# Warming TensorE on three float32 products and two gate products, with other cuts of the first two chunks

## The chip, the cores and the metric

The kernel runs on one core of one Trainium2 chip. The metric is the device time of one execution in microseconds. A product here is one matrix instruction of TensorE; the profile calls TensorE PE, VectorE DVE, ScalarE ACT, GpSimd POOL and SyncE SP.

## The reference

`x` has the shape (16, 2048, 1024), `w` (1024, 1024) and `decay` (1024), all float32. The kernel computes a matrix product and then a decaying running sum along the second axis:

```python
xw = x @ w
out[:, 0, :] = xw[:, 0, :]
for t in range(1, S):
    out[:, t, :] = decay[None, :] * out[:, t - 1, :] + xw[:, t, :]
```

## The kernel before

The 16 x 2048 rows of `x` are cut into 64 chunks of 512 rows (`TL`), and a chunk into 16 blocks of 32 rows (`NJ`). GpSimd's queue loads `x` in bfloat16 into tiles `xb`, one DMA for each of the four quadrants of 32 partitions (a quarter of the 1024 columns each). VectorE turns blocks of 32 x 32 pairs into `xw` (`turn`, L115), ScalarE or VectorE sorts them into `xt` (`part`, L123), and TensorE multiplies `xt`, or `xw` directly, with the weights `wsb` (`matmul`, L131). The products go to PSUM tiles `ps` and `spare`; the scan, the decays and the transposition back to the output follow on VectorE, ScalarE and GpSimd.

The work is a list of 264 steps, each of them one output tile: up to two chunks by 128 of the 1024 output columns. A table called `agenda` says which small pieces of work are issued in which step. Everything is pinned, so each engine runs its instructions in the order of the program. The entry -99 of the agenda is the beginning, before step 0. Its letters that matter here are `M` (load part of a chunk of `x`, `load_half`), `U` (load a part of `w`), `K` (`spin_on`), `E` (turn one part of a chunk), `F` and `G` (sort it), `w` and `W` (convert a piece of the weights into `wsb`, L326).

Chunks 0 and 1 are loaded, turned and multiplied in two parts each, so that TensorE can begin before a whole chunk has landed. `cuts` holds the borders: nine and seven blocks for chunk 0, eight and eight for chunk 1. For chunk 0, 32 products of 288 columns are followed by 32 of 224. The order on GpSimd's queue is: first part of chunk 0 (four DMAs), a quarter of `w`, the second part of chunk 0, chunk 1's two parts, the rest of `w`.

Before the first data are there, TensorE multiplies a cleared tile `idle` with itself, into the PSUM tile `spare`, whose content is overwritten later: 22 products at L344. After these come the gates: for each quadrant, ScalarE copies one landed column of `xb` into a cleared tile `gate` (L360), and TensorE multiplies with that gate three times (once for the last quadrant). Because of the copy, these products can't run before the quadrant's load has landed. The real products are queued behind them.

From step 40 to step 139 a no-op stands on TensorE's queue ahead of the products of each step.

Of the kernel before, what the change touches and what calls it, by code (L numbers as in the profile page):

```python
# [9 lines left out]
FP32 = mybir.dt.float32  # L10
BF16 = mybir.dt.bfloat16
# [14 lines left out]
def kernel(  # L26
# [26 lines left out]
    nc = tc.nc  # L53
    pin = tc.keep_in_program_order
    B, S, D = x.shape
    assert w.shape == (D, D)

    NQ = 4
    P = 32
# [3 lines left out]
    TL = 512  # L63
    NJ = TL // P
# [5 lines left out]
    const = ctx.enter_context(tc.tile_pool(name="const", bufs=1))  # L70
# [5 lines left out]
    def ring(pool, name, count, shape, dtype=FP32):  # L76
        i = turns[name] = turns.get(name, -1) + 1
        return pool.tile(shape, dtype, name=f"{name}{i % count}")

    def quad(q):  # L80
        return slice(q * P, (q + 1) * P)
# [17 lines left out]
    xt_of = {}  # L99
# [25 lines left out]
    def matmul(ps, n, k, xt, t0=0, t1=TL, start=0, pairs=None):  # L125
        if pairs is None:
            rhs = xt[:, k // 2, k % 2, t0:t1]
        else:
            rhs = pairs[:, k // 2, t0 // P:t1 // P, :, k % 2].rearrange("p j i -> p (j i)")
        lhs = wsb[:, k, n].rearrange("p q i -> p (q i)")  # L130
        pin(nc.tensor.matmul(  # L131
            out=ps[:, t0:t1] if ps.shape[1] >= t1 else ps,
            lhsT=lhs,
            rhs=rhs,
            start=(k == 0 and t0 == start),
            stop=(k == K - 1),
        ))
# [179 lines left out]
    def load_w(queues, h, e):  # L317
        for i, q in enumerate((0, 2, 1, 3)):
            pin(queues[i % len(queues)].dma_start(  # L319
                out=stage[h, e][quad(q)].rearrange("p (m d) -> p m d", m=M),  # L320
                in_=_ap(w, [[2 * D, P], [2 * P * D, M], [1, CH]],
                        (q * CQ + e) * D + h * CH)))
# [3 lines left out]
        pin(copy(out=wcols[:, 2 * m + e, h],  # L326
                 in_=src.rearrange("p (q r i) -> p q r i", q=NQ, r=R)))

    idle = const.tile([128, TL], BF16, name="idle")
    spare = ring(psp, "spare", 1, [128, TL])  # L330
    rows = const.tile([128, 2, P], FP32, name="rows")
    touch = const.tile([128, 1], BF16, name="touch")
    load_w((nc.sync, nc.scalar), 0, 0)
    pin(nc.vector.memset(idle, 0.0))  # L334
    pin(nc.vector.memset(rows, 0.0))
    pin(nc.scalar.copy(out=touch, in_=idle[:, 0:1]))

    gates = [const.tile([128, 128], BF16, name=f"gate{q}") for q in range(NQ)]
    for gate in gates:
        pin(nc.vector.memset(gate, 0.0))  # L340

    def spin(count, by):
        for _ in range(count):
            pin(nc.tensor.matmul(out=spare, lhsT=by, rhs=idle, start=True, stop=True))  # L344

    spin(22, idle[:, 0:128])
    H = NJ // 2
    cuts = (((0, H + 1), (H + 1, NJ)), ((0, H), (H, NJ)))
    for q in range(NQ):
        pin(nc.sync.dma_start(  # L350
            out=rows[q * P:q * P + R],
# [6 lines left out]

    def spin_on(q):
        pin(nc.scalar.copy(out=gates[q][quad(q), 0:1], in_=xb_of[0][quad(q), 0, 0:1]))  # L360
        spin(3 if q < NQ - 1 else 1, gates[q])

    def load_part(i):
        load_w((nc.gpsimd,), *((0, 1), (1, 0), (1, 1))[i])
# [42 lines left out]
    def finale():  # L407
        six, six_late = ring(psp, "ps", 3, [128, TL]), ring(psp, "ps", 3, [128, TL])
        seven, seven_late = ring(psp, "spare", 1, [128, TL]), ring(psp, "ps", 3, [128, TL])
        return tuple((early[:, 0:TL // 2], late[:, TL // 2:TL])  # L410
                     for early, late in ((six, six_late), (seven, seven_late)))

    def half_of(n, half, ks=range(K)):
        ps = finals[n % R - 2][half]
        t = half * (TL // 2)
        for k in ks:
            matmul(ps, n, k, xt_of[nch - 1], t, t + TL // 2, t)
# [49 lines left out]
    def turn_and_load(c):  # L467
# [40 lines left out]
        "L": lambda i: load(*loads.pop(0)) if loads else None,  # L508
    }
    agenda = {  # L510
        -99: "M0 U0 M1 M2 M3 U1 U2 w0 W1 w2 W3 K0 K1 K2 K3 E0 E1 G0 E2 G1 E3 F2 G3 W4 w5 W6 W7 D E4 E5 G4 E6 G5 E7 F6 G7 E8 E9 G8 E10 G9 E11 F10 G11 E12 L E13 G12 L E14 G13 E15 L F14 G15",
        0: "p0 z0 W8 W9 W10 W11",
        1: "g0",
        2: "L S1 L",
# [62 lines left out]
    def usual(s):  # L577
        paired = [t.paired for t in tiles]
        do = [f"P{s}"] if paired[s] else []
        if paired[s - 1]:  # L580
            do.append(f"S{s - 1}")
        if not paired[s]:
            do.append(f"S{s}")
        do.append(f"C{s - 1}")
        if paired[s - 2]:
            do.append(f"B{s - 2}")
        if not paired[s - 1]:
            do.append(f"B{s - 1}")
        return do + later.get(s, []) + ["L"] * (2 if len(loads) > NQ else 1)

    def rest(s):
        do = [f"S{s - 1}"] if tiles[s - 1].paired else []
        do.append(f"C{s - 1}")
        if tiles[s - 2].paired:
            do.append(f"B{s - 2}")
        return do + [f"B{s - 1}"] + later.get(s, []) + ["L"] * len(loads)

    def perform(do):
        for deed in do:
            deeds[deed[0]](int(deed[1:] or 0))  # L600
# [3 lines left out]
    for step, (g, n) in enumerate(slots):  # L604
        T = TL * len(g)
        left = step - len(slots)
        if n % R == 0:
            ns, nj = range(n, n + R), T // P
            if left == -2 * R:
                outlets = [Outlet(ns, H, half) for half in range(2)]  # L610
            else:
                pieces = 1 if left < -7 * R else 2 if left < -6 * R else nj // H
                outlets = [Outlet(ns, nj, pieces=pieces)]
        if left == -R:
            outlets = []
        if step == 0:
            heads = [ring(psp, "ps", 3, [128, T]) for _ in range(3)]
            firsts = [ps[:, 0:TL] for ps in heads] + [spares[0]]
            seconds = [ps[:, TL:T] for ps in heads] + [spares[1]]
            for j0, j1 in cuts[0]:  # L620
                for e in range(2):
                    for k in range(e, K, 2):
                        for i in range(R):
                            matmul(firsts[i], i, k, xt_of[0], j0 * P, j1 * P, j0 * P,
                                   pairs=None if e else xw_of[0])
            for k0 in range(0, K, 2):
                for i in range(R):
                    for k in (k0, k0 + 1):
                        matmul(seconds[i], i, k, xt_of[1], 0, H * P,
                               pairs=xw_of[1] if k0 < 4 else None)  # L630
            for i in range(R):
                for k in range(K):
                    matmul(seconds[i], i, k, xt_of[1], H * P, TL, H * P,
                           pairs=xw_of[1] if i < 2 else None)
        if step < R:
            ps = heads[n] if n < 3 else tuple(spares)
        else:
            if step == K + 1:
                ps = nexts
            elif left >= -2:  # L640
                finals = finals if left == -1 else finale()
                ps = finals[left + 2]
            elif len(g) == 2 or n % R < 3:
                ps = ring(psp, "ps", 3, [128, T])
            else:
                ps = ring(psp, "spare", 1, [128, TL])
            todo = [(k, l) for k in range(K) for l in range(len(g))]
            if step < K:
                todo.sort(key=lambda kl: kl[0] % 2)
            elif step == K:  # L650
                todo = []
                nexts = (ring(psp, "spare", 1, [128, TL]), ring(psp, "ps", 3, [128, T])[:, TL:T])
                for l in range(len(g)):
                    for i, one in enumerate((ps[:, l * TL:(l + 1) * TL], nexts[l])):
                        for k in range(K):
                            matmul(one, n + i, k, xt_of.get(g[l]),
                                   pairs=xw_of[g[l]] if l or not i and k >= M else None)
            elif step == K + 1:
                todo = []
            if left == -2:  # L660
                for m, half in ((n, 0), (n + 1, 0), (n, 1)):
                    half_of(m, half)
            if left >= -2:
                todo = []
            if 40 <= step < 140:
                pin(nc.tensor.nop(hint="room", nofuse=True))
            for k, l in todo:
                matmul(ps[:, l * TL:(l + 1) * TL], n, k, xt_of[g[l]])
        tiles.append(Tile(g, n, ps, outlets))
        do = agenda.get(step, agenda.get(left) if left >= -20 else None)  # L670
        if do is None:
            do = usual(step)
        else:
            do = do.split()
            if left == -20:
                do = rest(step) + do
        perform(do)
# [29 lines left out]
```

## Time and profile before

| | us |
|---|---|
| median of 3 runs | 904.14 |
| lowest and highest | 903.82, 904.59 |
| the profiled execution's own time | 903.76 |
| its span, from first to last instruction | 902.0 |
| first real product starts | 10.80 |
| last operation of TensorE ends | 897.94 |

| engine | busy us | share of the span |
|---|---|---|
| PE | 896.6 | 99% |
| DVE | 824.3 | 91% |
| ACT | 686.7 | 76% |
| POOL | 657.0 | 73% |

The span begins with the first instruction that the profile holds. Products overlap: one of 512 columns has a length of 0.379 us in the profile, but the next one starts 0.216 us after it. So the distance between starts is what says how fast TensorE works, and "busy" alone does not. A line of the timeline gives start, length, engine, line of the kernel, operation, what is written and read, the number of instructions merged, and in brackets the idle time of the engine ahead of it with what ended it. The granted clock is TensorE's, as a share of its full speed.

### The profile page before, as it was taken

The page shows a single profiled execution, that of the slowest core. Times are in us where ns is not written, and L with a number is a line of the kernel's source. Part 1 is how long each engine was busy: PE and PEld are TensorE (multiplying, and loading weights), DVE is VectorE, ACT ScalarE, POOL GpSimd, SP SyncE. Part 2 cuts the span into 40 slices and gives each one's busy share as a digit, 9 for nine tenths or more (in the row PEclk, how much of TensorE's full clock was granted, in tenths as well). Part 3 has the DMA queues.
Part 4 walks back from the last instruction along what each step waited for, and adds up shares of the span by engine and source line. Part 5 has one row for each costly group of instructions (what it writes and reads, how often), then busy time and mean ns, then how long its engine had stood idle before and what let it go on. Part 6 is the DMA issues. An engine that isn't in the chain of part 4 may idle for free.

```text
span 902.0 us, 12287 instructions
## 1 busy us (share of the span) xinstructions
PE 896.6 (99%) x4224; PEld 413.6 (46%) x4224; DVE 824.3 (91%) x633; ACT 686.7 (76%) x961; POOL 657.0 (73%) x756
## 2 busy tenths in 40 slices
PE   9999999999999999999999999999999999999998
PEld 6444444444444444444444444444444444444444
DVE  4999998998999999999998999999999999999998
ACT  4889867777877877878778778777787787787743
POOL 7988678777767768677677687777777776876532
PEclk9999999999999999999999999999999999999999
DMA  9999999999999999999999999999999999999858
GB/s 193 188 215 215 226 249 214 217 220 241 252 243 261 245 251 249 251 253 237 224 234 228 224 230 225 236 225 227 233 230 227 230 231 223 227 226 220 181 143 237
DMA packets 403182, 204.77 MB, mean 227 GB/s; under 512 B 9392, under 2 KB 402096, under 8 KB 403120
## 3 DMA queue, kind: packets, MB, share of 16 engines
q1 hardware_dynamic: 265808, 134.77, 60.7%
q0 software_dynamic: 137024, 68.70, 56.8%
q8 instruction: 33, 0.54, 0.2%
q10 hardware_dynamic: 288, 0.52, 0.2%
q14 instruction: 29, 0.24, 0.1%
HBM read 138.42 MB, written 134.22 MB: 302 GB/s over the span
## 4 chain that ended last, share of the span: by engine, by line
PE 98%; DMA 1%; POOL 0%; issue 0%; DVE 0%; DVEq 0%; POOLq 0%
PE ps L131 97%; DMA xb<-in_x_dram 1%; PE spare L131 1%; POOL xb L105 0%; PE spare L404 0%; PE ps L404 0%; DVE h L425 0%; DVE xw L115 0%; DVEq L702 0%; DVEq L115 0%; POOLq L691 0%
## 5 line engine op out<-in xcount | busy, mean ns | idle before, releaser
L131 PE MATMUL ps<-xt,wsb 128*128 128x512 bf16 (+1 forms) x4032 | 866.0, 377 | 0.0
L131 PEld LDWEIGHTS <-wsb 128*128 128x128 bf16 x4176 | 408.1, 98 | 477.3 <-ACT wsb L326 1.3
L205 POOL TENSOR_TENSOR xs<-h,xs 128x512 f32<-128x512 f32 (+1 forms) x190 | 242.7, 1278 | 185.5 <-ACT h L171 84.9
L278 DVE STREAM_TRANSPOSE ot<-so 128x1024 f32<-128x1024 f32 (+2 forms) x264 | 300.1, 1175 | 4.9 <-DMA out_dram<-ot 3.1
L191 ACT COPY xs<-ps 128x1024 f32<-128x1024 f32 (+1 forms) x190 | 188.8, 994 | 149.2 <-PE ps L131 142.6
L266 POOL TENSOR_TENSOR so<-h,xs 128x512 f32<-128x512 f32 (+1 forms) x189 | 240.3, 1273 | 43.8 <-ACT h L171 25.6
L123 ACT COPY xt<-xw 128x2048 bf16<-128x2048 bf16 (+3 forms) x136 | 242.2, 1789 | 8.0 <-DVE xw L115 7.9
L105 POOL DMA_DIRECT2D xb<-in_x_dram x264 | 174.2, 661 | 5.6 <-DMA xb<-in_x_dram 2.3
L171 ACT ACTIVATE h<-so,dec 128x512 f32<-128x512 f32 (+1 forms) x189 | 144.7, 767 | 30.6 <-DVE so L210 27.5
L115 DVE STREAM_TRANSPOSE xw<-xb 128x2048 f32<-128x2048 f32 (+3 forms) x78 | 147.4, 1901 | 7.4 <-DMA xb<-in_x_dram 7.4
L210 DVE TENSOR_TENSOR_SCAN so<-spare,keep,xs 128x512 f32<-128x512 f32 (+1 forms) x97 | 119.7, 1236 | 25.2 <-POOL xs L205 24.9
L210 DVE TENSOR_TENSOR_SCAN so<-spare,xs 128x512 f32<-128x512 f32 x93 | 113.2, 1219 | 26.5 <-POOL xs L205 23.6
L171 ACT ACTIVATE h<-ps,dec 128x512 f32<-128x512 f32 (+1 forms) x190 | 129.8, 683 | 0.0
L229 DVE TENSOR_TENSOR_SCAN so<-dec,ps 128x1024 f32<-128x1024 f32 x34 | 76.8, 2260 | 1.0 <-ACT h L171 1.0
L229 DVE TENSOR_TENSOR_SCAN so<-dec,keep,ps 128x1024 f32<-128x1024 f32 (+2 forms) x35 | 75.4, 2153 | 0.0
L270 ACT COPY keep<-so 128x1 f32<-128x1 f32 x136 | 25.3, 188 | 9.5 <-DVE so L229 9.0
L201 ACT COPY so<-keep 128x1 f32<-128x1 f32 x97 | 18.4, 191 | 2.7 <-DVE ot L278 2.5
L131 PE MATMUL spare<-xt,wsb 128*128 128x512 bf16 (+3 forms) x60 | 12.6, 329 | 0.0
L131 PE MATMUL ps<-xw,wsb 128*128 128x256 bf16 (+3 forms) x72 | 12.2, 306 | 0.1
L199 POOL MEMSET so<- 128x1 f32 x93 | 10.7, 116 | 0.6 <-DVE ot L278 0.6
L344 PE MATMUL spare<-idle 128*128 128x512 bf16 x22 | 7.6, 526 | 1.2 <-DVE idle L334 1.2
L319 POOL DMA_DIRECT2D ot<-in_w_dram x12 | 6.5, 545 | 0.9 <-issue 0.5
(41 smaller groups left out, 40.7 us busy)
## 6 DMA issues: line engine op xcount, KB each, us to landing
out_dram<-ot SPq DMA_DIRECT2D x236, 512.0 KB, 10.8
xb<-in_x_dram POOLq DMA_DIRECT2D x248, 256.0 KB, 7.9
out_dram<-ot SPq DMA_DIRECT2D x56, 128.0 KB, 2.5
out_dram<-ot SPq DMA_DIRECT2D x8, 256.0 KB, 4.3
ot<-in_w_dram POOLq DMA_DIRECT2D x12, 128.0 KB, 6.2
xb<-in_x_dram POOLq DMA_DIRECT2D x8, 128.0 KB, 4.6
out_dram<-xb SPq DMA_DIRECT2D x3, 256.0 KB
xb<-in_x_dram POOLq DMA_DIRECT2D x4, 144.0 KB, 6.5
```

Of the source, the lines that this page charges most:

```text
L105: pin(nc.gpsimd.dma_start(out=xb_of[c][quad(q), j0:j1], in_=_ap(x, [[D, P], [P * D, j1 - j0], [1, CQ]], (b * S + t0 + j0 * P) * D + q * CQ)))
L115: pin(nc.vector.transpose(out=dst.rearrange("p (m j i) -> p j m i", m=M, i=P)[:, j0:j1, m0:m1], in_=src.rearrange("p (j m c) -> p j m c", ...
L123: pin(copy(out=xt_of[c][:, m0:m1, :, j0 * P:j1 * P], in_=src))
L131: pin(nc.tensor.matmul(out=ps[:, t0:t1] if ps.shape[1] >= t1 else ps, lhsT=lhs, rhs=rhs, start=(k == 0 and t0 == start), stop=(k == K - 1),))
L171: pin(nc.scalar.activation(out=h[:, i * size:(i + 1) * size], in_=src, func=mybir.ActivationFunctionType.Copy, scale=dec[:, self.n:self.n ...
L191: pin(nc.scalar.copy(out=self.xs[:, i * size:(i + 1) * size], in_=ps))
L205: pin(nc.gpsimd.tensor_tensor(out=odds, in0=self.g, in1=odds, op=ALU.add))
L210: pin(nc.vector.tensor_tensor_scan(out=so[:, 3:T + 2:2], data0=squares[-1][:, n:n + 1].to_broadcast([128, T // 2]), data1=self.xs[:, 1:T:2 ...
L229: pin(nc.vector.tensor_tensor_scan(out=so[:, t + 2:t + 2 + size], data0=dec[:, n:n + 1].to_broadcast([128, size]), data1=ps, initial=befor ...
L266: pin(nc.gpsimd.tensor_tensor(out=self.so[:, 2:T + 2:2], in0=self.h, in1=self.xs[:, 0:T:2], op=ALU.add))
L270: pin(nc.scalar.copy(out=self.keep, in_=self.so[:, self.T + 1:self.T + 2]))
L278: pin(nc.vector.transpose(out=outlet.ot[:, :, c0:c0 + P], in_=self.so[:, 2 + t0:2 + t0 + nj * P].rearrange("p (i t) -> p i t", t=P)))
```

## The change

The 22 bfloat16 products on a cleared bfloat16 tile become three float32 products on a cleared float32 tile `wide`, twice as large. Of the four gates only those of the quadrants 1 and 3 stay, with one product each instead of three, three, three and one. Their right-hand side is the first half of `wide`, read as bfloat16. Chunk 0 is cut into ten and six blocks, chunk 1 into seven and nine; the number of products stays, their columns become 320 and 192, then 224 and 288. The no-ops reach to step 179.

```diff
-    idle = const.tile([128, TL], BF16, name="idle")
+    wide = const.tile([128, TL], FP32, name="wide")
+    idle = wide[:, 0:TL // 2].bitcast(BF16)
...
-    pin(nc.vector.memset(idle, 0.0))
+    pin(nc.vector.memset(wide, 0.0))
...
-    gates = [const.tile([128, 128], BF16, name=f"gate{q}") for q in range(NQ)]
-    for gate in gates:
+    gates = {q: const.tile([128, 128], BF16, name=f"gate{q}") for q in (1, 3)}
+    for gate in gates.values():
         pin(nc.vector.memset(gate, 0.0))

-    def spin(count, by):
+    def spin(count, by, on):
         for _ in range(count):
-            pin(nc.tensor.matmul(out=spare, lhsT=by, rhs=idle, start=True, stop=True))
-
-    spin(22, idle[:, 0:128])
+            pin(nc.tensor.matmul(out=spare, lhsT=by, rhs=on, start=True, stop=True))
+
+    spin(3, wide[:, 0:128], wide)
     H = NJ // 2
-    cuts = (((0, H + 1), (H + 1, NJ)), ((0, H), (H, NJ)))
+    cuts = (((0, H + 2), (H + 2, NJ)), ((0, H - 1), (H - 1, NJ)))
...
-        spin(3 if q < NQ - 1 else 1, gates[q])
+        spin(1, gates[q], idle)
...
-        -99: "M0 U0 M1 M2 M3 U1 U2 w0 W1 w2 W3 K0 K1 K2 K3 E0 E1 ...
+        -99: "M0 U0 M1 M2 M3 U1 U2 w0 W1 w2 W3 K1 K3 E0 E1 ...
...
+            Q = cuts[1][0][1] * P
             for k0 in range(0, K, 2):
                 for i in range(R):
                     for k in (k0, k0 + 1):
-                        matmul(seconds[i], i, k, xt_of[1], 0, H * P,
+                        matmul(seconds[i], i, k, xt_of[1], 0, Q,
                                pairs=xw_of[1] if k0 < 4 else None)
             for i in range(R):
                 for k in range(K):
-                    matmul(seconds[i], i, k, xt_of[1], H * P, TL, H * P,
+                    matmul(seconds[i], i, k, xt_of[1], Q, TL, Q,
                            pairs=xw_of[1] if i < 2 else None)
...
-            if 40 <= step < 140:
+            if 40 <= step < 180:
                 pin(nc.tensor.nop(hint="room", nofuse=True))
```

## The prediction

> **What bounds the kernel now.** I read the page's busy times and its chain first, then the timeline of the first 45 us, then tables of windows.
>
> The page: share of each engine, and the chain that ended last.
>
> ```profile
> PE 896.6 (99%) x4224; PEld 413.6 (46%) x4224; DVE 824.3 (91%) x633; ACT 686.7 (76%) x961; POOL 657.0 (73%) x756
> PE 98%; DMA 1%; POOL 0%; issue 0%; DVE 0%; DVEq 0%; POOLq 0%
> ```
>
> TensorE is the chain. So the change can act only through the moment at which real products begin, through TensorE's waits, and through its clock. The timeline (start, length, instruction, idle time before it) shows the beginning:
>
> ```profile
> 1.20 7.61 PE L344 MATMUL spare<-idle 128*128 128x512 bf16 x22 [1.20 <-DVE idle L334]
> ...
> 6.29 0.15 PEld L344 LDWEIGHTS <-idle 128*128 128x128 bf16 x1 [0.28 <-issue]
> 6.71 1.61 PEld L344 LDWEIGHTS <-idle 128*128 128x128 bf16 x8 [0.26 <-issue]
> ...
> 8.65 2.32 PE L344 MATMUL spare<-idle,gate 128*128 128x512 bf16 x10
> 8.71 0.19 ACT L360 COPY gate<-xb 32x1 bf16<-32x1 bf16 x1 [0.38 <-DMA xb<-in_x_dram]
> ...
> 10.02 0.19 ACT L360 COPY gate<-xb 32x1 bf16<-32x1 bf16 x1 [0.60 <-DMA xb<-in_x_dram]
> 10.07 1.56 DVE L115 STREAM_TRANSPOSE xw<-xb 128x288 f32<-128x288 f32 x4 [2.17 <-DMA xb<-in_x_dram]
> ...
> 10.80 0.54 PE L131 MATMUL ps<-xw,wsb 128*128 128x288 bf16 x3
> ```
>
> Until 6.7 us a spare product starts every 0.427 us, after that every 0.216 us: the clock rises at 6.68, which is where the trace's clock record begins to grant the whole clock. The ten gate products run without a break from 8.65 to 10.80, so they, and not the data, set the first real product: the first transposition ends at 10.07 + 0.45 = 10.52. The next waits, in the same view:
>
> ```profile
> 14.62 1.29 DVE L115 STREAM_TRANSPOSE xw<-xb 128x224 f32<-128x224 f32 x4 [1.07 <-DMA xb<-in_x_dram]
> 14.68 0.29 PE L131 MATMUL spare<-xt,wsb 128*128 128x288 bf16 x1
> ...
> 15.09 0.46 PE L131 MATMUL ps<-xw,wsb 128*128 128x224 bf16 x3
> ...
> 26.28 2.18 ACT L326 COPY wsb<-ot 128x512 bf16<-128x512 bf16 x4 [0.61 <-DMA ot<-in_w_dram]
> ```
>
> Products of 288 columns are 0.122 us apart, so the one at 14.68 is followed by 0.29 us of nothing: chunk 0's second part landed late. Weight loads alone, a little later:
>
> ```profile
> 27.99 0.11 PEld L131 LDWEIGHTS <-wsb 128*128 128x128 bf16 x2 [0.40 <-ACT wsb L326]
> 28.51 0.54 PEld L131 LDWEIGHTS <-wsb 128*128 128x128 bf16 x4 [0.41 <-ACT wsb L326]
> ```
>
> Here two product starts slip, by 0.07 and 0.08 us, because ScalarE's weight copies waited for the last weight DMA until 26.28. From 28.74 to 895 TensorE never waits. Two windows of 50 us, the first among the steps that already have a no-op, the second among those that get one (columns: PE busy and count, then the other engines, then granted clock):
>
> ```profile
> 250.00:300.00 50.00, 50.00 (x233) 22.66 (x232) 46.71 (x34) 39.31 (x53) 36.27 (x41) 1.00 1.23 249
> 550.00:600.00 50.00, 50.00 (x233) 22.67 (x232) 46.29 (x34) 38.88 (x51) 37.14 (x43) 1.00 1.19 230
> ```
>
> The clock at the end, in the same kind of table:
>
> ```profile
> 897.56:900.97 3.41, 0.38 (x4) 0.14 (x2) 0.76 (x2) 0.70 (x3) 0.00 (x0) 1.00 0.85 314
> 900.97:902.00 1.03, 0.00 (x0) 0.00 (x0) 0.00 (x0) 0.00 (x0) 0.00 (x0) 0.50 0.00 0
> ```
>
> TensorE's last operation ends at 897.94, the clock falls to half at 900.97: 3.03 us later.
>
> **The change, part by part.** The profiled execution took 903.76 us, 1.76 more than its span, and lies at the low end of the runs (903.82 to 904.59, median 904.14). Within 0.2% of that median (1.81 us, about what a measurement of this kernel can tell from no change) is 902.33 to 905.95.
>
> *No-ops.* Forty more, in steps 140 to 179. The trace has a hundred of 13 ns each, yet both windows above hold 233 products. Cost between 0 and 40 x 13 ns = 0.5 us; I take 0, because the existing ones hide behind queued products.
>
> *Memsets and ScalarE.* The idle tile's clearing took 0.27 us for 256 words; 512 words take about 0.54, so the first spare product moves from 1.20 to 1.47. Two clearings (0.11 each) and two gate copies (0.19 each) go away; ScalarE waited for DMA before three of its four copies, so nothing follows from that.
>
> *Ten blocks instead of nine.* Each of the four first loads grows by 16 KB as stored. The queue moves 196 GB/s between 8 and 14.6 us, so the fourth lands 4 x 16.4 / 196 = 0.33 us later and the second 0.17. The transposition starts at 10.40. Its length, by shape:
>
> ```profile
> L115 DVE STREAM_TRANSPOSE xw<-xb 128x288 f32<-128x288 f32 x4 | 1.6, 447 | 2.2 <-DMA xb<-in_x_dram 2.2
> L115 DVE STREAM_TRANSPOSE xw<-xb 128x224 f32<-128x224 f32 x4 | 1.3, 380 | 1.1 <-DMA xb<-in_x_dram 1.1
> ```
>
> For 320 columns that makes 0.48. From its end to TensorE took 0.09 us at 15.09 (14.62 + 0.38 = 15.00). So the data allow the first real product at 10.40 + 0.48 + 0.09 = 10.97, 0.17 later than now. The third gate's copy (10.35 to 10.54) and its one product end before or about then.
>
> *After that, at full clock.* The first part has 32 products, each 13.3 ns longer (32 more columns by the slope between 288 and 224): 4.00 + 0.43 = 4.43 us, ending at 15.40. The second part has the same bytes ahead of it, lands as now, and is ready at 15.05: the 0.29 us wait goes. It takes 3.13 - 0.43 = 2.70 and ends at 18.10 instead of 18.21. Chunk 1's first seven blocks land 0.33 us earlier (transposition at 17.01), its last nine as now (20.07), both ahead of need (18.10 and about 21.2); its two parts sum to the same 7.12 us. TensorE is therefore 0.11 us ahead at 25.2. What is late next is the weight copy above, held by a DMA that does not move: the 0.11 us are waited away by 28.74. Sum: between 0 and -0.11 us. The same wait also forgives: TensorE may be 0.11 + 0.15 = 0.26 us later than this before anything shows at the end.
>
> *The warm-up.* This is the uncertain term, since no float32 product is in the trace. The nearest rows are the float32 transpositions on TensorE at the end, beside bfloat16 products:
>
> ```profile
> 893.37 1.04 PE L131 MATMUL spare<-xt,wsb 128*128 128x256 bf16 x8
> ...
> 896.43 0.82 PE L404 MATMUL ps<-ident,so 128*128 128x128 f32 x6
> ```
>
> Both are 0.11 us apart, 256 columns against 128: float32 costs twice per column. A spare float32 product at half clock thus takes at least 2 x 0.427 = 0.85 us; if both operands of a true product are split so, twice again, 1.71 us, my estimate of the upper end. Three run from 1.47 to between 4.03 and 6.59. I take the upper end, because a transposition has data on one side only and a product has it on both. [...]
>
> Then TensorE is idle from 6.59 until the second load has landed: its copy, at 8.71 now, comes at 8.88 and ends at 9.07, the product starts near 9.15. That is 2.6 us without work, a product of 0.22, 1.2 us more, the second gate product, and the real work at 10.97. The cover that the ten gate products gave is gone, and whether the clock survives decides the outcome. The one fall in the trace came after 3.03 us without work; 2.6 is under that, so I forecast that the clock holds. Time: the median less about 0.1, **904.0**, own range 903.4 to 904.9.
>
> **The rivals.** *The clock falls in the gap* (slower). For it: the last 3.41 us before the fall held 0.38 us of TensorE work, 11%, and it fell all the same; any like stretch between 6.59 and 10.0 holds one gate product, 6%. Against: that work was transpositions, and no longest gap here reaches 3.03 us. Price: half clock from 10.97 until it rises again. It rose 5.48 us after the first product (1.20 to 6.68); with that, 5.48 / 2 - 0.26 = 2.5 us: 906.3. If it came back as quickly as it fell, 3.03 / 2 - 0.26 = 1.3: 905.0. It decides for "slower" where the half clock lasts over 4.5 us. [...]
>
> *The warm-up is too short, so the clock never rises before the real work.* For it: the lower end, 2.6 us of products ended by 4.03, against the 5.48 the present rise took. Against: the two-sided product. The price is the same, 905.0 to 906.3.
>
> *The real work starts earlier than I say.* If the loads did not slow and every wait went, the gain would be 0.19 (10.80 to 10.61) + 0.29 + 0.15 = 0.63 us: 903.5. For it: the gates do hold TensorE now. Against: the added bytes and the weight DMA. Even whole it stays within 0.2%; TensorE is full from 28.74 on, so nothing in the profile offers 1.8 us.
>
> **How the numbers follow.** Clock holds: 0.41. Earlier start: 0.03, within 0.2%, and 0.02 for a gain over 0.2% that I do not see. Clock falls: 0.35, of which 0.23 over 905.95. Warm-up too short: 0.19, of which 0.14 over 905.95. So faster 0.02; the same 0.41 + 0.03 + 0.12 + 0.05 = 0.61; slower 0.37. The range runs from 903.4 to 906.6: it takes in both cold cases' prices and most of the scatter of the runs.
>
> **What would show it.** Right: three products at L345 ending near 6.6, first real product near 10.97, real products of 320 columns about 0.14 us apart from the start, no gap before 192 columns, the weight-copy wait longer by 0.1. Wrong: real products 0.27 us apart (half clock), a clock record that begins after 11 us or has a break, spare products ending near 4, or a first transposition far from 10.4.

## The result and the profile after

The changed kernel takes 905.43 us (median of 22 runs, 904.44 to 906.26), the kernel before 904.06 (22 runs, 903.52 to 904.59). The ratio is 1.0014, 95% interval 1.0008 to 1.0020: slower by about 1.4 us, less than the 0.2% that was set as the limit, but more than the measurement's own uncertainty. The prediction was wrong in sign: 904.0 was forecast, a hair faster. The measured median lies inside the stated range.

The profiled execution of the changed kernel took 904.44 us, at the low end of its runs, 0.68 more than that of the kernel before. The page shows the same picture as before, TensorE as nearly the whole chain:

```profile
PE 894.0 (99%) x4200; PEld 412.1 (46%) x4200; DVE 825.6 (91%) x631; ACT 686.4 (76%) x959; POOL 656.8 (73%) x756
PE 98%; DMA 1%; POOL 0%; issue 0%; DVE 0%; ACT 0%; DVEq 0%; ACTq 0%; POOLq 0%
```

The timeline of the first 12 us:

```profile
1.46 5.33 PE L345 MATMUL spare<-wide 128*128 128x512 f32 x6 [1.46 <-DVE wide L335]
...
8.92 0.39 PE L345 MATMUL spare<-wide,gate 128*128 128x512 bf16 x1 [2.13 <-ACT gate L361]
...
10.09 1.69 DVE L115 STREAM_TRANSPOSE xw<-xb 128x320 f32<-128x320 f32 x4 [2.45 <-DMA xb<-in_x_dram]
...
10.29 0.61 PE L345 MATMUL spare<-wide,gate 128*128 128x512 bf16 x1 [0.98 <-ACT gate L361]
...
10.69 1.01 PE L131 MATMUL ps<-xw,wsb 128*128 128x320 bf16 x3
```

The three float32 products stand as six records, 0.853 us apart from the second on: 1.71 us for each product, the upper end of the estimate. The real work begins at 10.69. But its three merged products take 1.01 us: they are 0.267 us apart, nearly twice what 320 columns take at full clock (0.141 later in the same part). A table of windows, cut at the borders of the trace's clock record (window, length, PE busy and count, the other engines, then granted clock, DMA share, GB/s):

```profile
3.09:6.51 3.42, 3.42 (x5) 1.00 (x3) 0.00 (x0) 0.07 (x1) 2.87 (x6) 1.00 1.12 265
6.51:9.92 3.41, 0.67 (x2) 0.10 (x1) 0.76 (x2) 1.33 (x3) 1.59 (x3) 1.00 1.36 185
9.92:13.34 3.42, 3.05 (x11) 1.63 (x12) 3.02 (x9) 2.70 (x5) 3.07 (x6) 0.50 1.32 195
13.34:16.75 3.41, 3.41 (x28) 2.51 (x27) 1.80 (x8) 1.34 (x3) 3.41 (x7) 1.00 1.38 181
```

The clock rose at 6.51, fell at 9.92 and rose again at 13.34. (Ahead of the first rise the record is empty, and the table prints 1.00 there; the distances of the products say half: in the trace of the kernel before, 512 columns are 0.427 us apart ahead of its rise at 6.68 and 0.216 behind it.) Between the two rises lie two stretches of 3.41 us: the first with 0.67 us of TensorE work, the second at half clock with the real work in it.

The loss of this execution adds up. Real products ran at half clock from 10.69 to 13.34, 2.65 us; at 0.267 instead of 0.141 us each they lost 47% of that, 1.25. They began 0.11 earlier than before (10.69 against 10.80), the wait of 0.29 between chunk 0's parts is gone, and so are the 0.15 of the weight copies, which came in time for a later TensorE: 1.25 - 0.11 - 0.29 - 0.15 = 0.70. The last real product starts at 897.00 instead of 896.32, 0.68 later. From 28.7 on nothing differs; the window with the new no-ops holds 233 products as before:

```profile
550.00:600.00 50.00, 50.00 (x233) 22.69 (x232) 45.80 (x34) 38.86 (x52) 37.81 (x43) 1.00 1.19 231
```

The executions that were not profiled can be sorted as well, for every run's record has the mean granted clock over its span, in which the time ahead of the first rise counts as full (the kernel before has 0.999 with its first rise at 6.68 only; 6.68 us counted as half would have made it 0.996). In the 18 profiles of this study, a mean of 0.999 or 1.000 goes with no stretch of 3.41 us at half clock between the first rise and the end, 0.997 or 0.998 with one, 0.996 with two (a run at 0.995 is counted with these). The 22 runs of the changed kernel all lie between 0.995 and 0.998, the 113 runs of the kernel before that the experiments were compared with all at 0.999 or 1.000. By this sorting the clock rose and fell again in every run of the changed kernel: for one stretch in twelve of them (median 904.77), for two in ten (median 906.03).

### The profile page after: what moved, and what is told of

It is laid out like the page before. It is cut to its first block, busy times and chain, and to the rows that moved or that the text cites. A ratio compares the mean times of both kernels' runs of the same rounds, so it can differ in the third digit from the quotient of the medians.

```text
span 902.7 us, 12273 instructions
## 1 busy us (share of the span) xinstructions
PE 894.0 (99%) x4200; PEld 412.1 (46%) x4200; DVE 825.6 (91%) x631; ACT 686.4 (76%) x959; POOL 656.8 (73%) x756
## 4 chain that ended last, share of the span: by engine, by line
PE 98%; DMA 1%; POOL 0%; issue 0%; DVE 0%; ACT 0%; DVEq 0%; ACTq 0%; POOLq 0%
PE ps L131 97%; PE spare L131 1%; DMA xb<-in_x_dram 1%; POOL xb L105 0%; PE spare L405 0%; PE ps L405 0%; PE spare L345 0%; DVE h L426 0%; ACT gate L361 0%; DVEq L704 0%; ACTq L361 0%; POOLq L693 0%
## 5 line engine op out<-in xcount | busy, mean ns | idle before, releaser
L123 ACT COPY xt<-xw 128x2048 bf16<-128x2048 bf16 (+4 forms) x136 | 242.2, 1790 | 8.3 <-DVE xw L115 8.3
L115 DVE STREAM_TRANSPOSE xw<-xb 128x2048 f32<-128x2048 f32 (+4 forms) x78 | 147.3, 1900 | 7.1 <-DMA xb<-in_x_dram 7.1
L131 PE MATMUL ps<-xw,wsb 128*128 128x512 bf16 (+4 forms) x72 | 13.4, 325 | 0.0
L131 PE MATMUL spare<-xt,wsb 128*128 128x512 bf16 (+5 forms) x60 | 12.6, 330 | 0.0
L345 PE MATMUL spare<-wide 128*128 128x512 f32 x6 | 5.3, 1058 | 1.5 <-DVE wide L335 1.5
```

The costliest lines, as they stand in the source:

```text
L115: pin(nc.vector.transpose(out=dst.rearrange("p (m j i) -> p j m i", m=M, i=P)[:, j0:j1, m0:m1], in_=src.rearrange("p (j m c) -> p j m c", ...
L123: pin(copy(out=xt_of[c][:, m0:m1, :, j0 * P:j1 * P], in_=src))
L131: pin(nc.tensor.matmul(out=ps[:, t0:t1] if ps.shape[1] >= t1 else ps, lhsT=lhs, rhs=rhs, start=(k == 0 and t0 == start), stop=(k == K - 1),))
```

## The experiments

Theory 1: the clock falls because the stretch between warm-up and real work is almost empty. Theory 2: the warm-up of three float32 products is too short, so that many executions never see the rise. Theory 3: the new cuts cost the time. All ratios are against the kernel before, in runs on the same chip.

**Gate products put back** (a1_gates_full).

```diff
-    gates = {q: ... for q in (1, 3)}
+    gates = {q: ... for q in range(NQ)}
-        spin(1, gates[q], idle)
+        spin(3 if q < NQ - 1 else 1, gates[q], idle)
-        ... W3 K1 K3 E0 ...
+        ... W3 K0 K1 K2 K3 E0 ...
```

> The changed kernel with the ten gate products (three, three, three, one on four gates) put back. Theory 1 (gap): the clock falls because the stretch between the warm-up and the real work is almost empty; ten gate products fill it from about 8.3 on, the clock holds, 904.1 +- 0.3. Theory 2 (short warm-up): about 5.3 us of float32 products miss the rise in half of the executions; there ten gate products at half clock last 4.3 us, until 12.6 instead of 10.5, so the median stays at 905 or more and single times pass 906. Theory 3 (cuts): the ten-block first load costs the time, 905.4.

Measured: 904.77 (903.87 to 905.25), ratio 1.0009 [1.0000, 1.0017]. Neither figure of theory 1 nor of theory 2 fits in full, and the profile says why. There the clock rose early, at 4.43; the last four of the six float32 records took 2.43 us from 3.33 on, where four at 0.853 take 3.4, and ended by 5.8, 2.5 us before the first gate product at 8.26:

```profile
4.43:7.85 3.42, 1.33 (x3) 0.26 (x2) 0.76 (x2) 0.88 (x2) 1.53 (x3) 1.00 1.23 209
7.85:11.26 3.41, 3.00 (x8) 1.07 (x9) 1.10 (x3) 1.49 (x6) 2.62 (x5) 0.50 1.31 197
```

After 1.33 us of TensorE work in 3.42 us the clock fell too, and the gate products, now slow, held back the real work until 11.89. So the fall again came behind a stretch that was mostly empty, but that ten gate products fill it was wrong: the early rise made the warm-up itself shorter. The mean granted clock puts such a fall in five of the eleven runs.

**No gate products** (a2_no_gates): `K1 K3` taken out of the agenda.

> The changed kernel without any gate product: only three float32 products ahead of the real work. Theory 1 in its strict form (one or two products of 0.2 us count for nothing): 905.4 +- 0.3, as the changed kernel. If the two products do hold the clock in part of the executions: 906 or more. Theory 2: 905.4, since the warm-up is the same. Theory 3: 905.4.

Measured: 905.67 (904.81 to 906.51), 1.0019 [1.0009, 1.0028], 1.81 over the kernel before in the same runs. The changed kernel was 1.37 over it, and the two intervals overlap, so what the two lone products are worth, if anything, these runs cannot tell. In its profile the stretch from 6.79 to 10.20 holds nothing but the end of the warm-up, 0.14 us; the next one, with 2.53 us of TensorE work, was not followed by a rise, so two went by at half:

```profile
6.79:10.20 3.41, 0.14 (x1) 0.10 (x1) 0.76 (x2) 1.14 (x2) 1.52 (x3) 1.00 1.39 195
10.20:13.61 3.41, 2.53 (x10) 1.40 (x10) 2.93 (x9) 2.50 (x4) 3.07 (x6) 0.50 1.34 194
13.61:17.03 3.42, 3.42 (x15) 1.87 (x13) 1.88 (x8) 1.34 (x3) 3.42 (x7) 0.50 1.38 179
```

**A longer warm-up** (a3_five_f32).

```diff
-    spin(3, wide[:, 0:128], wide)
+    spin(5, wide[:, 0:128], wide)
```

> The changed kernel with five float32 products instead of three, two gate products as changed: products until about 8.3 (with the rise at 6.5) or 10.0 (without). Theory 1: the empty stretch shrinks from 3.8 us to under 2, the clock holds, 904.0 +- 0.3. Theory 2: the warm-up is long enough, 904.0 +- 0.3 too. Theory 3: still 905.4.

Measured: 904.25 (903.31 to 905.10), 1.0004 [0.9996, 1.0013]: most of the loss is gone with nothing but a later end of the warm-up. Single executions still lose; by the mean granted clock the clock fell in two of the eleven, and the profiled one (905.05) is such a case. Behind its stretch from 4.98 to 8.40, with 2.77 us of TensorE work, the clock held; behind the next, with 1.64, it fell at 11.81:

```profile
4.98:8.40 3.42, 2.77 (x7) 0.95 (x5) 0.76 (x2) 1.14 (x2) 1.27 (x3) 1.00 1.35 199
8.40:11.81 3.41, 1.64 (x9) 0.82 (x10) 1.45 (x4) 1.29 (x4) 2.68 (x6) 1.00 1.29 200
```

**bfloat16 instead of float32** (a4_twelve_bf16): `spin(12, idle[:, 0:128], idle)`.

> The changed kernel with twelve bfloat16 products of 0.427 us instead of three float32 products of 1.71 us: the same 5.1 us at half clock. Theories 1 and 2 both: 905.4 +- 0.4, as only the time counts. If float32 products count for less (or more) than bfloat16 ones in raising the clock, this differs: under 905.0 or over 905.8.

Measured: 905.55 (904.75 to 906.21), 1.0017 [1.0008, 1.0026], as the changed kernel (905.43); no difference between the types shows at the same time on TensorE. The mean granted clock (0.995 to 0.997) puts a fall in every run of this kernel, as it does in every run of the changed one (0.995 to 0.998), and a fall needs a rise ahead of it: a warm-up of 5.1 us was long enough in all of them. Theory 2 falls.

**The parts on the kernel before** (b1_cuts: new cuts alone; b2_two_gates: one product on the gates 1 and 3, 22 bfloat16 products kept; b3_f32: three float32 products instead of the 22, ten gate products; b4_nops: forty more no-ops).

> The kernel before with the new cuts alone (ten and six blocks, seven and nine), its own warm-up and its ten gate products. Theories 1 and 2: 904.0 +- 0.2, for the wait of 0.29 us between the parts goes and the weight copies take the rest back. Theory 3 (cuts): most of the loss of the changed kernel, 905.2.

> The kernel before with two gate products (quadrants 1 and 3, one each) instead of ten, its 22 bfloat16 products kept: they end near 8.7, 2 us before the real work. Theory 1: the stretch is short, the clock holds, and the real work can start up to 0.2 us earlier: 903.9 +- 0.2. Theory 2: the same. If lone gate products are too little even behind a long warm-up: 905 or more.

> The kernel before with three float32 products instead of its 22, ten gate products and the old cuts. Theory 1: the ten gate products begin near 8.3, the stretch without work is 1.5 us, the clock holds: 904.1 +- 0.3. Theory 2: the rise is missed in half of the executions and the gate products are then slow: 905 or more, with single times over 906.

> The kernel before with forty more no-ops on TensorE alone (steps 140 to 179). All theories: 904.06 +- 0.15. If each took its 13 ns from the products, 0.5 us more: 904.6.

| kernel | median us | lowest to highest | ratio, 95% interval |
|---|---|---|---|
| b1_cuts | 904.57 | 904.00 to 905.17 | 1.0006 [0.9997, 1.0015] |
| b2_two_gates | 904.10 | 904.04 to 904.61 | 1.0002 [0.9993, 1.0011] |
| b3_f32 | 904.25 | 903.72 to 904.93 | 1.0003 [0.9994, 1.0012] |
| b4_nops | 904.12 | 903.51 to 904.29 | 1.0000 [0.9991, 1.0009] |

The kernel before had 904.13 in these runs. No cost of the no-ops shows. Two gates instead of ten show none either behind 22 products; float32 products cost little in the median in front of ten gates. But theory 1's "the clock holds" was wrong for b3_f32 in part: in its profile (904.53) the clock fell at 7.90 and the real work began at 12.00 only, and the mean granted clock puts a fall in five of its eleven runs.

```profile
4.49:7.90 3.41, 1.30 (x3) 0.22 (x2) 0.74 (x2) 0.78 (x2) 1.54 (x3) 1.00 1.27 206
7.90:11.31 3.41, 2.90 (x7) 1.04 (x8) 1.42 (x5) 1.91 (x7) 2.68 (x5) 0.50 1.29 197
```

A fall in every run came only with both, a warm-up of 5.1 us and at most two gate products (the changed kernel, a2_no_gates, a4_twelve_bf16 and, below, d1_old_cuts); with ten gate products behind the short warm-up it came in five of eleven (a1_gates_full, b3_f32), with two behind the long one in one of eleven (b2_two_gates). In the profile of b2_two_gates the stretch ahead of the real work reads:

```profile
6.77:10.18 3.41, 2.35 (x12) 0.91 (x11) 1.01 (x3) 1.51 (x4) 1.88 (x4) 1.00 1.26 174
10.18:13.60 3.42, 3.08 (x22) 2.00 (x23) 2.57 (x10) 2.44 (x4) 3.04 (x6) 1.00 1.35 195
```

After these 2.35 us of TensorE work in 3.41 the clock held (1.00 in the next row). The cuts came out 0.44 over the kernel before; the interval takes in no change, so it needed more. In the profile of b1_cuts the clock held, but TensorE, done with chunk 1's first part at 21.35, waited 1.2 us for its second part:

```profile
22.55 0.65 PE L131 MATMUL ps<-xw,wsb 128*128 128x288 bf16 x3 [1.03 <-DVE xw L115]
```

**The stretch filled, with new and old cuts** (c1_filled, c4_filled_old_cuts): `spin(10, idle[:, 0:128], idle)` added behind the three float32 products of the changed kernel; the second with `cuts` as before.

> The changed kernel, its three float32 products and two gate products kept, with ten ungated bfloat16 products added behind the float32 ones; they reach to about 8.7. Theory 1 (a 3.41 us window that is mostly empty lowers the clock): the stretch without work shrinks from 3.8 to under 2 us, the clock holds in most executions and what is left over the kernel before is the cost of the cuts: 904.4 +- 0.3, single times from 903.8. Theory 2 (float32 warm-up misses the rise): 905 or more.

> As the kernel with the ten added products, and with the old cuts (nine and seven, eight and eight): the changed warm-up filled up, without the cuts. If the new cuts cost about 0.4: 904.0 +- 0.2, 0.4 under the one with the new cuts. If the cuts cost nothing: the same as that one.

Measured: 904.92 (903.49 to 905.20), 1.0007 [0.9998, 1.0016], and 904.15 (903.75 to 904.50), 1.0003 [0.9994, 1.0011]. With the old cuts the changed warm-up, filled up, is as good as the old one, as far as these runs can tell. With the new cuts it is not always. In that profile the clock fell at 11.15; with the old cuts it held:

```profile
7.73:11.15 3.42, 1.14 (x5) 0.40 (x5) 0.81 (x2) 0.84 (x4) 2.25 (x4) 1.00 1.28 188
11.15:14.56 3.41, 3.41 (x15) 1.90 (x13) 2.44 (x10) 2.33 (x4) 3.06 (x6) 0.50 1.40 193
```

```profile
6.07:9.48 3.41, 2.88 (x13) 0.98 (x10) 0.76 (x2) 1.33 (x3) 1.47 (x3) 1.00 1.34 184
9.48:12.89 3.41, 2.53 (x17) 1.54 (x17) 2.05 (x6) 2.19 (x5) 2.84 (x5) 1.00 1.32 195
```

The first real product came at 10.90 with the new cuts and at 10.18 with the old ones, but the stretches begin elsewhere too (7.73 and 6.07), so the two profiles do not show which of the two made the difference. The mean granted clock puts a fall in five of eleven runs with the new cuts and in none of eleven with the old.

**Each cut alone** (c2_cut_chunk0: ten and six blocks; c3_cut_chunk1: seven and nine).

> The kernel before with chunk 0 cut into ten and six blocks, chunk 1 as before. If the cost of the cuts is chunk 1's late second part: 904.1 +- 0.2, no loss. If it is the later first load: 904.5.

> The kernel before with chunk 1 cut into seven and nine blocks, chunk 0 as before. Chunk 1's second part is then needed 0.4 to 0.6 us earlier, while its load lands between 20 and 22 us from one execution to the next: 904.5 +- 0.2, as with both cuts. If the cost lies in chunk 0's first load: 904.1.

Measured: 903.95 for both (903.50 to 905.89 and 903.65 to 904.56), 1.0000 [0.9991, 1.0009] and 0.9997 [0.9989, 1.0006]. Neither alone shows a cost, so that chunk 1's second part is needed earlier is not enough.

**The changed kernel with the old cuts, and second looks** (d1_old_cuts; b1_cuts_again, c2_cut_chunk0_again, c3_cut_chunk1_again, one profile each).

> The changed kernel with the old cuts: three float32 products, two gate products, forty more no-ops, nine and seven, eight and eight blocks. Theory 1 with the cuts as a separate cost of about 0.4: 905.0 +- 0.3, a half clock at the first real product in every execution. If the cuts have no part in the loss: 905.4; if the warm-up has none: 904.1.

> A second look at the kernel before with both new cuts: if ten blocks at first bring the slow stretch of the GpSimd queue, its rate falls under 170 GB/s somewhere between 17 and 20 us, and chunk 1's second transposition begins after 20.3. If that was chance: 190 GB/s throughout and a start near 20.0.

> A second look at the kernel before with ten and six blocks for chunk 0: the slow stretch of the queue if ten blocks bring it, near 190 GB/s throughout if it was chance. The time is 904.0 +- 0.4 either way, since chunk 1's second part is needed at 21.6 only.

> A second look at the kernel before with seven and nine blocks for chunk 1: with nine blocks at first, near 190 GB/s from 14 to 24 us and a second transposition near 20.1; a slow stretch here would speak against ten blocks as its condition.

d1_old_cuts: 905.15 (904.46 to 905.71), 1.0008 [0.9999, 1.0017], against 904.20 for the kernel before. By the medians some 0.95 of the changed kernel's 1.37 us would be the warm-up's, and about 0.4 would go with the cuts, as b1_cuts said from the other side (0.44). That split is not shown: d1_old_cuts' interval takes in no change as well as the changed kernel's 1.0014. The mean granted clock puts a fall in all of its eleven runs. In the profile of d1_old_cuts the clock fell at 8.67, behind 0.92 us of TensorE work, and stayed at half for two stretches, the first of them with 2.59 us:

```profile
5.25:8.67 3.42, 0.92 (x2) 0.09 (x1) 0.76 (x2) 1.14 (x2) 1.29 (x3) 1.00 1.37 197
8.67:12.08 3.41, 2.59 (x9) 1.25 (x10) 1.90 (x5) 2.06 (x5) 3.13 (x7) 0.50 1.29 199
12.08:15.50 3.42, 3.42 (x16) 2.06 (x15) 2.15 (x10) 1.19 (x4) 3.42 (x7) 0.50 1.43 189
```

Its real products ran at half clock from 10.49 to 15.49, 5.0 us. By the working above that costs 2.37, less 0.31 for the earlier start, 0.29 and 0.15: 1.62. The profiled execution took 905.39, 1.63 more than that of the kernel before. So the loss of both profiles adds up without a term for the cuts. And in the changed kernel's profile TensorE did not wait for chunk 1's second part, because the half clock had made it late:

```profile
20.95 1.56 DVE L115 STREAM_TRANSPOSE xw<-xb 128x288 f32<-128x288 f32 x4 [1.86 <-DMA xb<-in_x_dram]
...
22.20 2.19 PE L131 MATMUL ps<-xw,wsb 128*128 128x288 bf16 x16
```

The second looks took 904.66 (both cuts), 903.81 (chunk 0's) and 904.21 (chunk 1's), one execution each. In b1_cuts_again the load queue again slowed between 17.5 and 19.0 us; c3_cut_chunk1_again, below it, shows the usual rate:

```profile
17.50:19.00 1.50, 1.50 (x19) 1.46 (x17) 0.94 (x4) 1.32 (x3) 1.07 (x3) 1.00 1.33 158
```

```profile
17.50:19.00 1.50, 1.50 (x18) 1.48 (x16) 1.28 (x5) 1.34 (x3) 1.20 (x3) 1.00 1.44 191
```

So the last nine blocks of chunk 1 were turned at 20.82, and TensorE waited 0.3 us for them (the weight copies behind them on the queue came later too, at 26.95 instead of 26.28):

```profile
20.82 1.56 DVE L115 STREAM_TRANSPOSE xw<-xb 128x288 f32<-128x288 f32 x4 [2.39 <-DMA xb<-in_x_dram]
...
21.36 1.37 PE L131 MATMUL ps<-xw,wsb 128*128 128x288 bf16 x7
21.36 1.17 PEld L131 LDWEIGHTS <-wsb 128*128 128x128 bf16 x7 [0.29 <-issue]
```

In the eight profiles with both new cuts (the changed kernel among them) this transposition begins at 19.96 to 22.02, median 20.9; in the ten others at 19.97 to 20.64, median 20.2. Whether ten blocks alone bring the slow stretch isn't settled. Between 17.5 and 19.0 us the queue moved 106 to 170 GB/s in seven of the ten profiles with ten blocks first, and 183 to 193 in all eight with nine. With ten blocks for chunk 0 alone it was 170 in c2_cut_chunk0 and 187 in c2_cut_chunk0_again. Shown is that with both cuts the landing is late in five of eight profiles (after 20.64), and that it meets an earlier need (21.1 to 21.4 in the two profiles of the kernel before with both cuts, 21.4 to 21.8 with one cut or none, ten gates and a clock that held). Why the queue slows, while all its loads have long been issued, stays open.

No experiment points to a version that beats the kernel before: with two gates b2_two_gates starts the real work at 10.46 instead of 10.80, and ends the same, since the later loads and the weight copies take it back. (With ten gates b4_nops started at 10.43, so the earlier start is not shown to be the gates' doing.)

## Why the prediction was wrong, point by point

- **No-ops, memsets, gate copies** at nothing: right (904.12 with the no-ops alone).
- **The first real product at 10.97**: it came at 10.69 in the changed kernel's profile and at 10.80 to 11.08 in four others where only the data held it. The 0.33 us were right: the first transposition begins at 10.25 in the median of ten profiles with ten blocks, at 9.92 in that of eight with nine.
- **Float32 product, 1.71 us**: right, 2 x 0.853.
- **"The one fall in the trace came after 3.03 us without work; 2.6 is under that, so I forecast that the clock holds"**: this is the step that failed. In the changed kernel's profile the clock fell although TensorE's longest time without work there was 2.13 us, and a3_five_f32 shows a fall behind a stretch of which at most 1.77 us were without (3.41 less 1.64 busy). How much work a stretch holds would have told more: in the rows printed here the clock fell behind stretches of 3.41 us with 0.14 to 1.64 us of TensorE work, the changed kernel's with 0.67 among them, and held behind those with 1.81 to 2.88. The one with 1.81 stands at the end of b1_cuts_again, mostly float32 transpositions:

```profile
896.79:900.20 3.41, 1.81 (x17) 1.50 (x15) 1.96 (x4) 1.79 (x5) 0.00 (x0) 1.00 0.97 310
900.20:902.87 2.67, 0.00 (x0) 0.00 (x0) 0.00 (x0) 0.00 (x0) 0.00 (x0) 1.00 0.43 163
```

The row that told this stood in the prediction as the argument for the rival: 0.38 us, 11%, in the last 3.41 us before the fall.
- **The rival "the clock falls in the gap"**: right; the clock fell at 9.92, between the two gate products. Its price of 1.3 to 2.5 us over the kernel before was bounded at the low end by the time of a fall; measured was 1.37 in the median and 0.4 to 2.2 over the single runs. The times that the prediction gives for it, 905.0 and 906.3, are added to 903.76, the profiled execution's; on the median of 904.14 they are 905.4 and 906.6. Real work met half clock for 2.65 us in the changed kernel's profile and for 5.0 in that of d1_old_cuts, a loss of 1.25 and 2.37 by the working above, of which the removed waits and the earlier start give back 0.55 in the first and 0.75 in the second.
- **The rival "the warm-up is too short"**: wrong; the changed kernel's profile has its first rise at 6.51, and the mean granted clock (0.995 to 0.998) puts a fall, and so a rise ahead of it, in each of the 22 runs.
- **The cuts at 0 to -0.11**: no loss shows for each alone; the two together came out 0.44 over on the kernel before, at the edge of what its runs can tell. The step "its last nine as now (20.07)" failed: with both cuts they are turned at 20.9 in the median, 0.7 later than in the other profiles. In the changed kernel's profile that cost nothing, since TensorE came to them at 22.20 only.
- **The forgiveness of 0.26 us** was right in kind: the weight-copy wait vanished in the changed kernel.

## What to carry to other kernels

The prediction compared the longest gap with the one gap behind which it had seen the clock fall, 3.03 us; the clock then fell behind a gap of 2.13. Spare products that are to keep TensorE's clock up are better judged by the clock record, and by how much TensorE work each stretch ahead of the real work holds, for an early rise as well as for a late one: in a1_gates_full the rise came at 4.43 instead of 6.51 and the warm-up ended by 5.8, and ten gate products did not make up for it. Where the rise differs from run to run, compare distributions: one profile shows one case of several. A cut that moves work ahead of a load must be held against the spread of that load's landing, not against its time in one profile.

## What the runs showed of the hardware

The changed kernel's clock record changes at 6.51, 9.92 and 13.34, 3.413 us apart both times; that distance is the length of the stretches below. The rows with the granted clock behind them:

| profile | stretch, us | TensorE busy, us | granted clock behind it |
|---|---|---|---|
| a2_no_gates | 6.79 to 10.20 | 0.14 | 0.50 |
| before, at its end | 897.56 to 900.97 | 0.38 | 0.50 |
| after | 6.51 to 9.92 | 0.67 | 0.50 |
| d1_old_cuts | 5.25 to 8.67 | 0.92 | 0.50 |
| c1_filled | 7.73 to 11.15 | 1.14 | 0.50 |
| after, at its end | 897.38 to 900.80 | 1.23 | 0.50 |
| b3_f32 | 4.49 to 7.90 | 1.30 | 0.50 |
| a1_gates_full | 4.43 to 7.85 | 1.33 | 0.50 |
| a3_five_f32 | 8.40 to 11.81 | 1.64 | 0.50 |
| b1_cuts_again, at its end | 896.79 to 900.20 | 1.81 | 1.00 |
| b2_two_gates | 6.77 to 10.18 | 2.35 | 1.00 |
| a3_five_f32 | 4.98 to 8.40 | 2.77 | 1.00 |
| c4_filled_old_cuts | 6.07 to 9.48 | 2.88 | 1.00 |

At half clock, a stretch with 2.53 us of TensorE work (a2_no_gates, 10.20 to 13.61) and one with 2.59 (d1_old_cuts, 8.67 to 12.08) were followed by another at 0.50; one with 3.05 (the changed kernel, 9.92 to 13.34) by 1.00. These are the rows of single executions: whether the work in a stretch is what decides, and where the line would lie, they do not show.

The first rise came at 6.68 in the kernel before, at 6.51 in the changed kernel and at 4.43 in a1_gates_full; what sets it, no run here shows. The 22 runs of the changed kernel spread over 1.8 us, one stretch at half clock in twelve of them and two in ten by their mean granted clock, those of the kernel before over 1.1.
